# A copy by ScalarE between two products of a Strassen-like down projection

## The chip, the core and the metric

The kernel runs on one core of a Trainium2 chip. The metric is the device time of one execution in microseconds (us); for a kernel that was run several times the median stands. Matmuls run on TensorE (PE in the profile), elementwise work on VectorE (DVE) and ScalarE (ACT), and loads from HBM are issued by SyncE (SP).

## The reference

A decoder trunk for 512 tokens of width 1024, two layers, everything in float32. Each layer is: half an FFN, a mixer (gated linear attention in the first, stick-breaking attention in the second), half an FFN. There are four FFNs, and the change lies in them alone:

```python
D_MODEL, SEQ, DEPTH, D_FF = 1024, 512, 2, 2816

def swiglu(h, w_gate, w_up, w_down):
    return (jax.nn.silu(h @ w_gate) * (h @ w_up)) @ w_down

def reference(x, ...):
    for i in range(DEPTH):
        x = x + 0.5 * swiglu(rmsnorm(x, ffn1_norm[i]), ffn1_w_gate[i], ffn1_w_up[i], ffn1_w_down[i])
        ...  # mixer, added to x
        x = x + 0.5 * swiglu(rmsnorm(x, ffn2_norm[i]), ffn2_w_gate[i], ffn2_w_up[i], ffn2_w_down[i])
    return rmsnorm(x, final_norm)
```

## The kernel before

The residual x lies transposed in SBUF as eight tiles of 128 features by 512 tokens (`xs`). Each float32 operand of a matmul is cut into a high and a low part (`wh`, `wl` for weights): ScalarE casts the high part (L127), VectorE subtracts it to get the low part (L129), and three matmuls (high by high, low by high, high by low) replace one.

An FFN works through its 2816 inner features in six groups. For most of them the gate and up projections (`seven`, matmuls at L689), and for one group the down projection (`seven_down`, matmuls at L368), are done by a scheme with seven half-size products in place of eight (Winograd's form of Strassen's): sums of weight quarters (`sums_12`, `sums_34`; L672 to L679 in `seven`, L352 to L360 in `seven_down`) are multiplied with sums of quarters of the other factor. Other groups go through a plain `down` (tiles `ps_d`).

`seven_down` is called twice in each FFN, as part 0 and part 1 (256 of each 512 output features), so eight times in all. Its two bodies go through seven products, each for m = 0 and m = 1 (128 features each) and each made of 6 matmuls of 128x256. Products are summed in PSUM in six banks: ws[m], zs[m] and qs[m]. After each product but the first (t1, t2 and so on), `add` (L374) has VectorE read the sum from PSUM, scale it by 0.5 and add it into a quarter of the residual. The sum in ws goes on after that: `body_1` puts the product with b11 there, a copy of it goes to zs (L386, ScalarE), then the product with t2 is added; `body_2` adds the product with t3, then works on qs with b22, and then adds the product with t4 to ws. Between t3 and t4 the sum is needed once, for `add(m, 1, 1, ...)`, and a matmul into ws[m] may not start until that has read it.

In `seven` the corresponding sum after t3 is first copied by ScalarE into a tile `u3` in SBUF (L731, tag "c", one buffer), and VectorE adds from there (L732).

The program's order: a queue (`feed`) of entries. At the start of an entry the weights of the next entries are cut as far as four wide buffers allow, and raw weights are loaded up to six entries ahead into two buffers (`raw`, `rawd`). A load into such a buffer starts when the last reader of its former contents is done, which is often the cut of the last quarter (a22, L129 with 128x512). Each engine takes its instructions in order; the order on each is set when the program is built, by a scheduler with its own estimate of times. For the first column block of a `seven` entry that follows other work, ScalarE makes a small cast of 128x128 (L134). Behind `seven_down` part 0 come two pairs of `seven` entries (gate and up); behind part 1 comes a `down`.

Of the kernel before, what the change touches and what calls it, by code (L numbers as in the profile page):

```python
# [10 lines left out]
F32 = mybir.dt.float32  # L11
# [7 lines left out]
P = 128  # L19
# [13 lines left out]
def decoder(ctx: ExitStack, tc: tile.TileContext, a: dict, out: bass.AP):  # L33
    nc = tc.nc
# [12 lines left out]
    def psum(name, tag=None):  # L47
        if tag is None:
            tag = order[turn_[0] % 8]
            turn_[0] += 1  # L50
        return pp.tile([P, T], F32, tag=tag, bufs=banks[tag], name=name)
# [280 lines left out]
    def seven_down(pool, w, r0, hs, part):  # L332

        H = T // 2
        lower, upper = (
            Chunk(w[r0 : r0 + 4 * P, c : c + 256].rearrange("(f p) c -> p f c", p=P), 4, 256)
            for c in (part * 256, 512 + part * 256)
        )  # L340
        lower.few = upper.few = True
        v = {}

        def halves():

            lo, up = (c.load().rearrange("p (c two) d -> p two c d", two=2) for c in (lower, upper))
            return lo[:, 0], lo[:, 1], up[:, 0], up[:, 1]

        def sums_12(_):
            a11, _, a21, a22 = halves()  # L350
            s = v["s12"] = pool().tile([P, 4, 256], F32, tag="s", bufs=4, name="s12")
            nc.vector.tensor_tensor(out=s[:, 0:2], in0=a21, in1=a22, op=ALU.add)  # L352
            nc.vector.tensor_tensor(out=s[:, 2:4], in0=s[:, 0:2], in1=a11, op=ALU.subtract)
            return s

        def sums_34(_):
            a11, a12, a21, _ = halves()
            s = pool().tile([P, 4, 256], F32, tag="s", bufs=4, name="s34")
            nc.vector.tensor_tensor(out=s[:, 0:2], in0=a11, in1=a21, op=ALU.subtract)
            nc.vector.tensor_tensor(out=s[:, 2:4], in0=a12, in1=v["s12"][:, 2:4], op=ALU.subtract)  # L360
            return s

        def prod(ps, w, k0, step, m, b, first):
            for c in range(2):
                bh, bl = hs[c][b]
                wh, wl = (t[:, k0 + step * c, m * P : (m + 1) * P] for t in w)
                for n, (l_, r_) in enumerate(((wh, bh), (wl, bh), (wh, bl))):
                    st["pe"] = nc.tensor.matmul(  # L368
                        ps, l_, r_, start=first and c + n == 0, stop=c == 1 and n == 2, skip_group_check=True
                    ).ins  # L370

        def add(m, up, col, ps):
            x = xs[part * 2 + m + 4 * up][:, col * H : col * H + H]
            nc.vector.scalar_tensor_tensor(out=x, in0=ps, scalar=0.5, in1=x, op0=ALU.mult, op1=ALU.add)  # L374

        def body_1(W):
            ax, s = W
            ws, zs, qs = [], [], []
            for m in range(2):
                ws.append(psum("ps_w")[:, 0:H])  # L380
                prod(ws[m], ax, 0, 2, m, "b11", True)
            for m in range(2):


                zs.append(psum("ps_z")[:, 0:H])
                nc.scalar.copy(zs[m], ws[m])  # L386
            yield
            for m in range(2):
                qs.append(psum("ps_q")[:, 0:H])
                prod(qs[m], s, 0, 1, m, "t1", True)  # L390
                add(m, 1, 1, qs[m])
            yield
            for m in range(2):
                prod(ws[m], s, 2, 1, m, "t2", False)
                add(m, 0, 1, ws[m])
            yield
            for m in range(2):
                prod(zs[m], ax, 1, 2, m, "b21", False)
                add(m, 0, 0, zs[m])
            v["w"], v["q"] = ws, qs  # L400
            yield

        def body_2(W):
            s, a22 = W
            ws, qs = v["w"], v["q"]
            for m in range(2):
                prod(ws[m], s, 0, 1, m, "t3", False)
                add(m, 1, 1, ws[m])
            yield
            for m in range(2):  # L410
                prod(qs[m], s, 2, 1, m, "b22", False)
                add(m, 0, 1, qs[m])
            yield
            for m in range(2):
                prod(ws[m], a22, 0, 1, m, "t4", False)
                add(m, 1, 0, ws[m])
            yield

        feed.q.append(
            Entry([(lower, lambda t: t, 4, 256), (lower, sums_12, 4, 256)], body_1, NEAR, feed.q[-1].place != NEAR)  # L420
        )
        assert not feed.q[-1].lead
        feed.q.append(Entry([(lower, sums_34, 4, 256), (upper, lambda t: halves()[3], 2, 256)], body_2, NEAR))

    def back_tok(w, r0, nf, hs, done):
# [1165 lines left out]
```

## Time and profile before

| | |
|---|---|
| time, median of 3 runs | 1854.52 us (1854.33 to 1854.69) |
| the profiled execution's own time | 1856.01 us |
| its span, first to last instruction | 1854.0 us |
| mean granted TensorE clock | 0.999 |
| TensorE busy | 1828.8 us (99%) |
| VectorE busy | 1476.4 us (80%) |
| ScalarE busy | 1035.9 us (56%) |
| updates of `seven_down` (L374) | 96 on VectorE, 48 of them from ps_w |

Rows of the timeline give the start and the duration of an instruction in us, its engine, its line, the operation, output<-input by tile names with shapes, and in brackets how long the engine sat idle before it and what ended that. A matmul's duration overlaps that of the next: matmuls of 128x256 are issued one after another at much shorter distance than they last. Rows of the groups give the busy time in us, the mean duration in ns, the idle time before and what ended it. The chain of waits is followed back from the last instruction of the span.

### The profile page before, as it was taken

What the parts mean: (1) busy time and instruction counts of PE and PEld (TensorE: products, weight loads), DVE (VectorE), ACT (ScalarE), POOL (GpSimd) and SP (SyncE); (2) the same over time, 40 slices, a digit from 0 to 9 for tenths busy, and PEclk for the clock granted to TensorE, in tenths of its full rate; (3) what the DMA queues carried; (4) which work ended last, traced back from release to release, by engine and by line L of the source; (5) the groups of instructions that cost most, each with busy time, mean ns of one, the idle gap of its engine ahead of it and who ended that gap; (6) DMA issues with size and microseconds to landing.
All of it is one profiled execution on the core that took longest, in us unless ns stands there. A gap on an engine that the chain in (4) does not pass through costs nothing.

```text
span 1854.0 us, 29888 instructions
## 1 busy us (share of the span) xinstructions
PE 1828.8 (99%) x12187; PEld 1649.6 (89%) x12187; DVE 1476.4 (80%) x2336; ACT 1035.9 (56%) x1771; POOL 8.7 (0%) x20
## 2 busy tenths in 40 slices
PE   7999999999999999999999999999999999999998
PEld 6999999889888899999889999998888788999997
DVE  7998776785787989877798997676878779997775
ACT  6555445444555565545565555455878755654454
POOL 0000000100000000000000000000000000000000
PEclk9999999999999999999999999999999999999999
DMA  5333333311223223332233333232221222333321
GB/s 160 114 125 95 118 110 100 98 57 62 69 69 114 91 92 115 115 114 87 82 128 104 98 118 107 95 92 85 69 69 59 67 91 93 112 125 97 121 80 69
DMA packets 177613, 179.16 MB, mean 97 GB/s; under 512 B 4098, under 2 KB 167988, under 8 KB 177476
## 3 DMA queue, kind: packets, MB, share of 16 engines
q1 hardware_dynamic: 176768, 176.18, 30.1%
q8 instruction: 95, 1.56, 0.4%
q0 software_dynamic: 608, 1.05, 0.2%
q14 instruction: 42, 0.34, 0.1%
q10 hardware_dynamic: 100, 0.03, 0.0%
HBM read 175.17 MB, written 2.10 MB: 96 GB/s over the span
## 4 chain that ended last, share of the span: by engine, by line
PE 86%; DVE 9%; DMA 3%; ACT 2%; issue 1%; SPq 0%; DVEq 0%; ACTq 0%
PE ps_d L67 20%; PE ps_f L67 18%; PE ps_w L689 17%; PE ps_q L689 9%; PE ps_t L67 5%; PE ps_z L689 4%; PE ps_b L67 4%; DVE wl L129 3%; DMA raw<-in_ffn_w_gate_dram 2%; PE ps_S L67 1%; PE ps_z L1315 1%; PE ps_bt L67 1%; PE ps_oT L1377 1%; PE ps_w L368 1%; DVE x L374 1%
## 5 line engine op out<-in xcount | busy, mean ns | idle before, releaser
L129 DVE TENSOR_TENSOR wl<-raw,wh 128x1024 fp32r<-128x1024 f32 (+1 forms) x244 | 259.2, 1066 | 89.3 <-ACT wh L127 50.1
L127 ACT CAST wh<-raw 128x1024 fp32r<-128x1024 f32 (+1 forms) x244 | 224.7, 923 | 160.4 <-PE ps_d L67 45.4
L689 PE MATMUL ps_w<-th,wh 128*128 128x256 f32 x864 | 239.6, 277 | 1.4 <-ACT o L719 0.6
L689 PE MATMUL ps_w<-tl,wh 128*128 128x256 f32 x864 | 238.7, 276 | 0.0
L689 PE MATMUL ps_w<-th,wl 128*128 128x256 f32 x864 | 238.6, 276 | 0.0
L129 DVE TENSOR_TENSOR wl<-s,wh 128x1024 fp32r<-128x1024 f32 x160 | 195.4, 1222 | 54.0 <-PE ps_z L689 37.4
L127 ACT CAST wh<-s 128x1024 fp32r<-128x1024 f32 x160 | 168.0, 1050 | 116.8 <-PE ps_d L67 28.9
L67 PE MATMUL ps_d<-hh,wl 128*128 128x512 f32 x544 | 212.1, 390 | 0.0
L67 PE MATMUL ps_d<-hh,wh 128*128 128x512 f32 x544 | 212.1, 390 | 0.0
L67 PE MATMUL ps_d<-hl,wh 128*128 128x512 f32 x544 | 211.6, 389 | 0.0
L67 PE MATMUL ps_f<-xh,wh 128*128 128x512 f32 x448 | 178.9, 400 | 1.6 <-ACT wh L127 1.6
L67 PE MATMUL ps_f<-xl,wh 128*128 128x512 f32 x448 | 175.8, 393 | 0.0
L67 PE MATMUL ps_f<-xh,wl 128*128 128x512 f32 x448 | 175.1, 391 | 0.0
L689 PEld LDWEIGHTS ps_w<-th,wh 128*128 128x128 f32 x864 | 162.3, 188 | 3.0 <-ACT u L731 1.0
L689 PEld LDWEIGHTS ps_w<-th,wl 128*128 128x128 f32 x864 | 162.2, 188 | 0.0
L689 PEld LDWEIGHTS ps_w<-tl,wh 128*128 128x128 f32 x864 | 162.2, 188 | 0.0
L127 ACT CAST wh<-rawd 128x1024 fp32r<-128x1024 f32 (+1 forms) x84 | 84.9, 1012 | 120.3 <-PE ps_d L67 77.4
L323 DVE SCALAR_TENSOR_TENSOR x<-ps_d,x 128x512 f32<-128x512 f32 x152 | 102.9, 688 | 58.6 <-PE ps_d L67 58.0
L129 DVE TENSOR_TENSOR wl<-rawd,wh 128x1024 fp32r<-128x1024 f32 (+1 forms) x84 | 98.3, 1174 | 42.4 <-ACT wh L127 25.1
L67 PEld LDWEIGHTS ps_d<-hl,wh 128*128 128x128 f32 x544 | 102.1, 188 | 21.6
L67 PEld LDWEIGHTS ps_d<-hh,wh 128*128 128x128 f32 x544 | 102.1, 188 | 20.2
L67 PEld LDWEIGHTS ps_d<-hh,wl 128*128 128x128 f32 x544 | 102.1, 188 | 19.7
(323 smaller groups left out, 4847.9 us busy)
## 6 DMA issues: line engine op xcount, KB each, us to landing
raw<-in_ffn_w_gate_dram SPq DMA_DIRECT2D x43, 1024.0 KB, 5.4
raw<-in_ffn_w_up_dram SPq DMA_DIRECT2D x43, 1024.0 KB, 5.4
rawd<-in_ffn_w_down_dram SPq DMA_DIRECT2D x84, 512.0 KB, 3.7
raw<-in_gla_w_in_dram SPq DMA_DIRECT2D x12, 1024.0 KB, 5.3
raw<-in_sb_w_in_dram SPq DMA_DIRECT2D x16, 512.0 KB, 3.8
raw<-in_gla_w_out_dram SPq DMA_DIRECT2D x4, 1024.0 KB, 5.0
raw<-in_sb_w_in_dram SPq DMA_DIRECT2D x4, 1024.0 KB, 5.1
raw<-in_sb_w_out_dram SPq DMA_DIRECT2D x4, 1024.0 KB, 5.0
```

What stands on the lines that cost most here:

```text
L67: st["pe"] = nc.tensor.matmul(ps, l, r, start=first, stop=last).ins
L127: st["cut"] = nc.scalar.copy(h, r).ins
L129: nc.vector.tensor_tensor(out=l, in0=r, in1=h.bitcast(F32), op=ALU.subtract)
L323: nc.vector.scalar_tensor_tensor(out=xs[k], in0=ps, scalar=0.5, in1=xs[k], op0=ALU.mult, op1=ALU.add)
L368: st["pe"] = nc.tensor.matmul(ps, l_, r_, start=first and c + n == 0, stop=c == 1 and n == 2, skip_group_check=True).ins
L374: nc.vector.scalar_tensor_tensor(out=x, in0=ps, scalar=0.5, in1=x, op0=ALU.mult, op1=ALU.add)
L689: st["pe"] = nc.tensor.matmul(o, l_, r_, start=first and j + n == 0, stop=j == 3 and n == 2, skip_group_check=True).ins
L1315: nc.tensor.matmul(o_, l_, r_, start=first, stop=last, skip_group_check=True)
L1377: nc.tensor.matmul(po[e * 64 : e * 64 + 64, j * P : T], self.v[j][:, c : c + 64], self.wt[p, e][bk][:, c0 : c0 + n], start=j == 0, stop=j ...
```

## The change

In `body_2` of `seven_down`, after the product with t3, ScalarE copies the sum from PSUM into a tile `u3` in SBUF, and the update of the residual by VectorE reads `u3`. The tile has two halves, one for each m, and takes the buffer with tag "c" that `seven` uses for its own `u3`; that buffer becomes twice as large. In the built program sixteen copies are added to ScalarE's queue, at each call both together, behind the cast of weight sums that stood there and ahead of the next cast. The t4 matmuls wait for ScalarE where they waited for VectorE. On VectorE the number of instructions is the same; in part 0 of each FFN one sum of weights of the next `seven` (L678), which stood between the two updates that follow t4, is placed later: behind both updates and the next cut (L129, 128x512) in FFNs 1, 3 and 4, behind the two updates and ahead of that cut in FFN 2. TensorE's and SyncE's order is unchanged.

```diff
         def body_2(W):
             s, a22 = W
             ws, qs = v["w"], v["q"]
+
+            u3 = pool().tile([P, 2, H], F32, tag="c", bufs=1, name="u3")
             for m in range(2):
                 prod(ws[m], s, 0, 1, m, "t3", False)
-                add(m, 1, 1, ws[m])
+                nc.scalar.copy(u3[:, m], ws[m])
+                add(m, 1, 1, u3[:, m])
             yield
             for m in range(2):
                 prod(qs[m], s, 2, 1, m, "b22", False)
                 add(m, 0, 1, qs[m])
             yield
             for m in range(2):
                 prod(ws[m], a22, 0, 1, m, "t4", False)
                 add(m, 1, 0, ws[m])
             yield
```

## Prediction

> **What bounds the kernel now.** I read the page first, then TensorE's own waits, then the timelines of the three compute engines around one call of `seven_down`, then the chain of waits behind it. The page's busy times:
>
> ```profile
> PE 1828.8 (99%) x12187; PEld 1649.6 (89%) x12187; DVE 1476.4 (80%) x2336; ACT 1035.9 (56%) x1771; POOL 8.7 (0%) x20
> ```
>
> TensorE sets the time. All that an edit on VectorE or ScalarE can give is a pause of TensorE, so its waits come next (total us, times, longest):
>
> ```profile
> PE ps_w L368 <- DVE x L374: 5.4, 8, 1.1
> ...
> PE ps_w L689 <- ACT u L731: 0.4, 2, 0.2
> ```
>
> L368 is the matmul of `seven_down` and L374 its residual update. There are eight calls (four FFNs, parts 0 and 1), and each pauses once. Where, the first call shows (start, duration of TensorE's matmuls):
>
> ```profile
> 146.41 0.28 PE L368 MATMUL ps_w<-t,wh 128*128 128x256 f32 x1
> ...
> 147.77 0.28 PE L368 MATMUL ps_q<-hl,wh 128*128 128x256 f32 x1
> 149.08 0.38 PE L368 MATMUL ps_w<-nh,wh 128*128 128x256 f32 x1 [1.03 <-DVE x L374]
> 149.30 0.28 PE L368 MATMUL ps_w<-nh,wl 128*128 128x256 f32 x1
> ```
>
> The third product (t3 into ps_w) ends at 146.7, the one with b22 (into ps_q) is issued until 147.77, and the one with t4, which goes on summing in ps_w, starts at 149.08: it may not write before VectorE has read the sum behind t3. VectorE at that time:
>
> ```profile
> 148.00 0.70 DVE L673 TENSOR_TENSOR s<-s,raw 128x512 f32<-128x512 f32 x1
> 148.60 0.76 DVE L374 SCALAR_TENSOR_TENSOR x<-ps_w,x 128x256 f32<-128x256 f32 x2
> 149.26 0.76 DVE L374 SCALAR_TENSOR_TENSOR x<-ps_q,x 128x256 f32<-128x256 f32 x2
> 150.07 0.42 DVE L374 SCALAR_TENSOR_TENSOR x<-ps_w,x 128x256 f32<-128x256 f32 x1
> 150.41 0.68 DVE L678 TENSOR_TENSOR s<-raw 128x512 f32<-128x512 f32 x1
> ...
> 151.40 0.69 DVE L129 TENSOR_TENSOR wl<-raw,wh 128x512 fp32r<-128x512 f32 x1
> ```
>
> The read that TensorE needs comes 1.9 us after its sum was ready, because VectorE is behind with weights (L673 here). ScalarE in the same stretch is not behind:
>
> ```profile
> 145.37 1.05 ACT L127 CAST wh<-s 128x1024 fp32r<-128x1024 f32 x1 [0.26 <-PE ps_z L368]
> 148.13 1.04 ACT L127 CAST wh<-raw 128x1024 fp32r<-128x1024 f32 x1 [1.71 <-PE ps_q L368]
> 150.75 0.62 ACT L127 CAST wh<-raw 128x512 fp32r<-128x512 f32 x1 [1.57 <-PE ps_w L368]
> ```
>
> It idles from 146.42 to 148.13, until b22's product is done.
>
> **The change, part by part.** *The copies.* Sixteen are added (8 calls, m = 0 and 1). The groups of instructions (busy us, mean ns, idle before) hold the nearest rows:
>
> ```profile
> L323 DVE SCALAR_TENSOR_TENSOR x<-ps_d,x 128x512 f32<-128x512 f32 x152 | 102.9, 688 | 58.6 <-PE ps_d L67 58.0
> ...
> L732 DVE TENSOR_TENSOR o<-u,o 128x256 f32<-128x256 f32 x72 | 30.3, 421 | 0.0
> L735 DVE TENSOR_TENSOR o<-ps_q,o 128x256 f32<-128x256 f32 x72 | 30.2, 420 | 0.0
> L473 DVE SCALAR_TENSOR_TENSOR xl<-x,gT,xh 128x512 fp32r<-128x512 f32 x40 | 29.8, 747 | 7.3 <-ACT xh L472 7.3
> ...
> L731 ACT COPY u<-ps_w 128x256 f32<-128x256 f32 x72 | 26.9, 373 | 14.8 <-PE ps_w L689 12.6
> ```
>
> L731 is the same copy in the same shape: 16 x 0.373 = 6.0 us of ScalarE. In the built order both copies of a call stand right behind the cast at 145.37 and ahead of the one at 148.13 (in part 1 likewise between two casts). So in the first call copy m = 0 runs from 146.42 to 146.8 and m = 1, whose product ends at 146.69, to about 147.15. The t4 product could start at 147.77 + 0.11 = 147.88, so copy m = 0 is 1.1 us early, and m = 1, needed 0.7 us later, 1.4 us. What is queued behind them on ScalarE is the cast at 148.13, which waits for TensorE anyway; nothing waits for that. Cost: nothing on the path. Without this idle time the copies would take up to 0.75 us per call.
>
> *The update.* It now reads SBUF. Bounds: no change, by L732 against L735 (421 and 420 ns, SBUF and PSUM source, same shape), and 0.06 us more, which is what the same kind of instruction takes longer with all its operands in SBUF (L473, 747 ns) than with one in PSUM (L323, 688 ns; both 512 columns). I take no change: L732 has the update's shape and operands and differs only in the scale, where L473 reads its scale from a tile and writes another type. Upper end 16 x 0.06 = 1 us of VectorE. The Trainium skill ("Perfetto Trace Analysis", Optimizing Scalar/DVE Operations) gives VectorE some 60 ns of access overhead on SBUF against 125 ns on PSUM, and by it the updates would get cheaper; L732 and L735 do not show that.
>
> *The wait.* TensorE's t4 product now waits for the copy instead of the update, and the copy is early, so the eight pauses go. A pause costs more than its idle time: without it the second t4 matmul would be issued two issue steps of 0.113 us (1.36 us for 12, below) after 147.77, at 148.00, and it is issued at 149.30: 1.30 us for 1.03 of idle, 0.27 more. All eight: 5.4 + 8 x 0.27 = 7.6 us. The four of part 1 are the short ones, 0.60, 0.18, 0.18 and 0.35; the first and the last:
>
> ```profile
> 189.76 0.38 PE L368 MATMUL ps_w<-nh,wh 128*128 128x256 f32 x1 [0.60 <-DVE x L374]
> ...
> 1678.83 0.39 PE L368 MATMUL ps_w<-nh,wh 128*128 128x256 f32 x1 [0.35 <-DVE x L374]
> ```
>
> Part 1 is 1.31 + 4 x 0.27 = 2.4 us, part 0 the other 5.2 us.
>
> *What is late next.* Behind part 0 TensorE meets a second wait, some 19 us on. In the chain that ended last it reads, in the second FFN (start, duration):
>
> ```profile
> 726.18 5.42 DMA raw<-in_ffn_w_gate_dram
> ...
> 736.55 5.45 DMA raw<-in_ffn_w_up_dram
> ...
> 742.23 0.38 ACT u L731
> 742.60 0.04 issue
> 742.65 3.01 PE ps_w L689 x24
> 745.65 1.36 PE ps_q L689 x12
> ```
>
> The cut of the a22 weights (L129, 128x512) frees a raw buffer; that starts a gate load; VectorE's sums of it and the next cut free another buffer for an up load; ScalarE's small cast of that (L134) stands ahead of copy L731 in its queue, and TensorE waits for L731. In the other FFNs the same cast waits for the same load; the first and the last of the four:
>
> ```profile
> 167.71 0.30 ACT L134 CAST w<-raw 128x128 fp32r<-128x128 f32 x1 [0.95 <-DMA raw<-in_ffn_w_up_dram]
> ...
> 1658.52 0.30 ACT L134 CAST w<-raw 128x128 fp32r<-128x128 f32 x1 [1.06 <-DMA raw<-in_ffn_w_up_dram]
> ```
>
> So TensorE is held there already, and what part 0 wins is kept only as far as this chain starts earlier. It starts with the cut at 151.40. Today that waits for ScalarE's cast at 150.75, which waits for the t4 product. With t4 done 1.3 us earlier the cast ends by 150.1, and VectorE decides: its backlog isn't shortened. Behind the ps_q updates (149.26 + 0.76, less the 0.09 by which neighbours overlap) it is free at 149.93; two t4 updates of 0.33 net bring it to 150.6. In the built order L678, which stands between the two t4 updates today, has moved behind the cut in FFNs 1, 3 and 4, so the cut starts at 150.6, 0.80 us earlier than today. In FFN 2 L678 only moves behind the second update and stays ahead of the cut; 0.60 us of the 0.80 is gone and 0.2 is left. Kept of part 0: 3 x 0.80 + 0.2 = 2.6 of 5.2 us.
>
> Behind part 1 come 24 matmuls of a `down`, during which VectorE and ScalarE wait for TensorE; the chain starts anew from TensorE's time there, and I keep all 2.4 us.
>
> *Sum.* 2.6 + 2.4 = 5.0 us. The profiled execution took 1856.0 us with a span of 1854.0; it would come to 1851.0 and 1849.0. It lies 1.5 us above the median of 1854.5, from which the forecast is 1849.5 us, 0.27% less. Some 0.2%, 3.7 us, is what a measurement here can tell from no change.
>
> **The rivals.** *Full gain.* If the loads are not what holds the up cast (a transfer that lands earlier once fewer are in flight), TensorE keeps 7.6 us: 1846.9. Against it is that the chain of waits runs through both loads without slack. 0.10.
>
> *Given back.* VectorE's work does not shrink, and in these stretches it is the engine that is behind. If the weight cuts that follow hold TensorE by what it came early, or the update from SBUF costs its 0.06 us and the cut moves that much less, part 0 keeps nothing and the gain is part 1's at most: 1852.1, down to nothing, 1854.5. For it: the backlog in the VectorE rows. Against it: the list of TensorE's waits names no wait on a weight cut of these stretches, so the cuts have room. 0.24. The Trainium skill ("VectorE: DVE Perf Modes", Rules for kernel authors) points this way: it has a matmul's output copied to SBUF first only if many operations follow, and here one does; by that rule alone the sum would be 0. The rule weighs VectorE's time, while the rows have TensorE waiting for the PSUM bank.
>
> *Slower: copies behind the cast.* If the copies reached ScalarE behind the cast at 148.13, that waits for b22's product and takes 1.04 us, t4 could start only at 148.13 + 1.04 + 0.37 = 149.5, 0.4 us later than today, and in part 1, where a pause costs 2.4 / 4 = 0.6 us and not 1.3, by the same geometry 1.1 us later: 4 x 0.4 + 4 x 1.1 = 6 us, 1860.5. It decides from the point where copy m = 0 ends more than its 1.1 us later than worked out above, and makes the kernel slower from 2.4 us later in part 0 (1.1 + 1.3) and 1.7 in part 1 (1.1 + 0.6). The built order speaks against it. With whatever else keeps ScalarE busy before t3's end, 0.10.
>
> That the change doesn't do what it says is excluded by the built program: t4's first matmuls wait for ScalarE there, and no longer for VectorE.
>
> **How the numbers follow.** The forecast, 1849.5, has 0.56, with 1848.2 to 1850.8 as its own range (the 0.80 us of FFNs 1, 3 and 4 taken as uncertain by 0.3 each, and part of the 1 us of VectorE). The range for 8 in 10 takes in the full gain, 1846.9, and the part-1-only case up to 1852.8; left out are the slower case and the half of "given back" that ends close to today's time. Faster by over 0.2% (under 1850.8): 0.56 + 0.10 = 0.66; within: 0.24; slower: 0.10.
>
> **What would show it.** Right: TensorE's list of waits has no entry L368 on the update; t4 follows b22 at one issue step; sixteen copies of about 0.37 us in ScalarE's idle time; the wait on L731 19 us behind part 0 has grown from 0.4 us to about 3 us in all (by the 2.6 us that part 0 doesn't keep); the a22 cut stands 0.8 us closer behind the t3 product in three FFNs and 0.2 in one. Wrong: an L368 wait on the copy; no longer L731 wait and 7 us gained; or new waits of TensorE on L129 in place of the old ones.

## Result and the profile after

| | before | after |
|---|---|---|
| median, beside each other on one chip (7 runs each) | 1854.52 us (1853.08 to 1855.45) | 1848.36 us (1846.99 to 1850.55) |
| ratio after / before, 95% interval | | 0.9968 [0.9957, 0.998] |
| the profiled execution's own time, its span | 1856.01, 1854.0 us | 1849.38, 1847.5 us |

The change makes the kernel faster by 3.7 to 8.0 us (by the interval), 6.2 us by the medians; repeated on another chip (below) it gave 0.9972 [0.9962, 0.9982], 4.5 us by the medians. The forecast was 1849.5 us. Lines behind 404 have moved by 3: L731 of before is L734 of after, L689 is L692, L678 is L681. The copy is L410.

The busy times of after, from the page, and TensorE's waits (total us, times, longest us):

```profile
PE 1827.2 (99%) x12187; PEld 1649.9 (89%) x12187; DVE 1475.1 (80%) x2336; ACT 1040.5 (56%) x1787; POOL 8.7 (0%) x20
...
PE ps_w L692 <- ACT u L734: 2.3, 4, 0.7
...
PE ps_w L692 <- ACT ps_z L716: 0.6, 3, 0.2
...
PE ps_w L368 <- ACT ps_z L386: 0.3, 1, 0.3
```

VectorE's busy time is nearly that of before (1475.1 against 1476.4 us), ScalarE has 16 instructions more, and TensorE executes as many matmuls as before. The entry `L368 <- DVE x L374` (5.4 us in 8) is gone, and none on L410 has come. In its place the wait at the copy in `seven` has grown from 0.4 us in 2 to 2.3 us in 4, one in each FFN. TensorE in the first call, part 0 of the first FFN (start, duration):

```profile
146.98 0.28 PE L368 MATMUL ps_q<-hh,wl 128*128 128x256 f32 x1
147.09 0.28 PE L368 MATMUL ps_q<-hl,wh 128*128 128x256 f32 x1
147.21 0.28 PE L368 MATMUL ps_w<-nh,wh 128*128 128x256 f32 x1
147.32 0.28 PE L368 MATMUL ps_w<-nh,wl 128*128 128x256 f32 x1
```

The product with t4 (ps_w) follows the one with b22 (ps_q) at one issue step. ScalarE and VectorE in the same stretch:

```profile
145.64 0.78 ACT L410 COPY u<-ps_w 128x256 f32<-128x256 f32 x2
147.41 1.05 ACT L127 CAST wh<-raw 128x1024 fp32r<-128x1024 f32 x1 [0.99 <-PE ps_q L368]
148.76 0.62 ACT L127 CAST wh<-raw 128x512 fp32r<-128x512 f32 x1 [0.31 <-PE ps_w L368]
```

```profile
147.95 0.75 DVE L374 SCALAR_TENSOR_TENSOR x<-u,x 128x256 f32<-128x256 f32 x2
...
149.29 0.75 DVE L374 SCALAR_TENSOR_TENSOR x<-ps_w,x 128x256 f32<-128x256 f32 x2
149.95 0.68 DVE L129 TENSOR_TENSOR wl<-raw,wh 128x512 fp32r<-128x512 f32 x1
150.55 0.69 DVE L681 TENSOR_TENSOR s<-raw 128x512 f32<-128x512 f32 x1
```

Both copies lie in ScalarE's idle time and are over at 146.42, 0.79 us before t4's first matmul. VectorE reads `u` only at 147.95, so its read, had TensorE still to wait for it, would hold t4 as before. The cut (L129, 128x512) starts at 149.95, with L681 behind it. In the second FFN L681 stands ahead of the cut:

```profile
721.49 0.68 DVE L681 TENSOR_TENSOR s<-raw 128x512 f32<-128x512 f32 x1
722.09 0.68 DVE L129 TENSOR_TENSOR wl<-raw,wh 128x512 fp32r<-128x512 f32 x1
```

The groups of instructions of after (busy us, mean ns):

```profile
L410 ACT COPY u<-ps_w 128x256 f32<-128x256 f32 x16 | 5.9, 368 | 0.6 <-PE ps_w L368 0.3
```

```profile
L374 DVE SCALAR_TENSOR_TENSOR x<-ps_w,x 128x256 f32<-128x256 f32 x32 | 12.3, 411 | 0.0
...
L374 DVE SCALAR_TENSOR_TENSOR x<-u,x 128x256 f32<-128x256 f32 x16 | 6.0, 415 | 0.0
```

And 19 us behind that call, ScalarE and then TensorE:

```profile
166.47 0.30 ACT L134 CAST w<-raw 128x128 fp32r<-128x128 f32 x1 [1.69 <-DMA raw<-in_ffn_w_up_dram]
166.68 0.36 ACT L734 COPY u<-ps_w 128x256 f32<-128x256 f32 x1
```

```profile
167.09 0.39 PE L692 MATMUL ps_w<-th,wh 128*128 128x256 f32 x1 [0.69 <-ACT u L734]
```

The small cast L134 waits for the up load (1.69 us, before: 0.95), the copy L734 stands behind it, and TensorE, earlier than before, now idles 0.69 us there.

How long each of the eight calls of `seven_down` takes on TensorE, from the start of its first L368 matmul to that of its last, is read off the timelines (us):

| trace | part 0: FFN 1, 2, 3, 4 | part 1: FFN 1, 2, 3, 4 |
|---|---|---|
| before | 10.70, 10.82, 10.70, 10.82 | 11.83, 9.87, 9.87, 10.04 |
| after | 9.41, 9.41, 9.41, 9.41 | 10.37, 9.41, 9.41, 9.85 |

84 matmuls, issued 0.1133 us apart, take 9.4 us from first to last. In part 0 the four calls became shorter by 1.29, 1.41, 1.29 and 1.41 us, 5.40 in all. Part 1 of the first FFN holds another wait, for a late load, in both traces (last section).

### The profile page after: what moved, and what is told of

The parts are those of the page before. It is cut to its first block, busy times and chain, and to the rows that moved or that the text cites. A ratio compares the mean times of both kernels' runs of the same rounds, so it can differ in the third digit from the quotient of the medians.

```text
span 1847.5 us, 29912 instructions
## 1 busy us (share of the span) xinstructions
PE 1827.2 (99%) x12187; PEld 1649.9 (89%) x12187; DVE 1475.1 (80%) x2336; ACT 1040.5 (56%) x1787; POOL 8.7 (0%) x20
## 4 chain that ended last, share of the span: by engine, by line
PE 89%; DVE 5%; DMA 3%; ACT 1%; issue 1%; SPq 0%; ACTq 0%; DVEq 0%
PE ps_d L67 20%; PE ps_w L692 18%; PE ps_f L67 18%; PE ps_q L692 9%; PE ps_t L67 5%; PE ps_z L692 5%; PE ps_b L67 4%; DVE wl L129 2%; PE ps_w L368 2%; DMA raw<-in_ffn_w_gate_dram 2%; PE ps_S L67 1%; PE ps_z L1318 1%; PE ps_bt L67 1%; DMA raw<-in_ffn_w_up_dram 1%; PE ps_oT L1380 1%; PE ps_T L1365 1%
## 5 line engine op out<-in xcount | busy, mean ns | idle before, releaser
L129 DVE TENSOR_TENSOR wl<-raw,wh 128x1024 fp32r<-128x1024 f32 (+1 forms) x244 | 258.2, 1062 | 89.8 <-ACT wh L127 56.4
L692 PE MATMUL ps_w<-th,wh 128*128 128x256 f32 x864 | 239.6, 277 | 2.9 <-ACT u L734 2.3
L692 PE MATMUL ps_w<-tl,wh 128*128 128x256 f32 x864 | 238.8, 276 | 0.0
L692 PE MATMUL ps_w<-th,wl 128*128 128x256 f32 x864 | 238.7, 276 | 0.0
L129 DVE TENSOR_TENSOR wl<-s,wh 128x1024 fp32r<-128x1024 f32 x160 | 195.0, 1220 | 50.4 <-PE ps_z L692 34.7
L692 PEld LDWEIGHTS ps_w<-th,wh 128*128 128x128 f32 x864 | 162.3, 188 | 4.4 <-ACT u L734 3.1
L692 PEld LDWEIGHTS ps_w<-tl,wh 128*128 128x128 f32 x864 | 162.3, 188 | 0.0
L692 PEld LDWEIGHTS ps_w<-th,wl 128*128 128x128 f32 x864 | 162.2, 188 | 0.0
L129 DVE TENSOR_TENSOR wl<-rawd,wh 128x1024 fp32r<-128x1024 f32 (+1 forms) x84 | 98.0, 1170 | 41.7 <-ACT wh L127 24.1
```

What stands on the lines that cost most here:

```text
L129: nc.vector.tensor_tensor(out=l, in0=r, in1=h.bitcast(F32), op=ALU.subtract)
L692: st["pe"] = nc.tensor.matmul(o, l_, r_, start=first and j + n == 0, stop=j == 3 and n == 2, skip_group_check=True).ins
```

## Experiments

The theory: TensorE gains because its t4 product no longer waits until VectorE has read the PSUM bank; it keeps all of that in part 1, and in part 0 only as much as the chain of cut, gate load, up load and small cast L134 starts earlier. Rivals: VectorE gains because it reads SBUF; the copies cost ScalarE time on the path; the second wait doesn't bind; what part 0 keeps comes from the other place of one weight sum in VectorE's order (L678 of before), and not from the bank.

**The copies are made and not read.**

```diff
-                add(m, 1, 1, u3[:, m])
+                add(m, 1, 1, ws[m])
```

> The changed kernel, but the update behind t3 reads the sum in PSUM again; ScalarE's sixteen copies are still made and nobody reads them. VectorE's order is that of the kernel before. Bank release (my theory: the gain is TensorE no longer waiting for VectorE's read of ps_w ahead of t4): the eight pauses L368 <- DVE x L374 are back (about 5.4 us of idle), the sixteen copies take 6 us of ScalarE's idle time and cost nothing, and the time is that of the kernel before, within 1 us; the list of TensorE's waits again has about 0.4 us on the copy in seven. Cheaper update (the gain comes from VectorE reading SBUF): also the time of before. So this run by itself tells what the copies cost: if they cost anything, it is above before by up to 6 us. Copies behind the cast (the slower rival of the prediction) would show as a wait L368 <- ACT u L410.

Measured: 1853.31 us against 1854.66 for before on that chip, ratio 0.9995 [0.9987, 1.0004]. TensorE's waits, and the group of the copies:

```profile
PE ps_w L368 <- DVE x L374: 4.2, 6, 1.0
...
PE ps_w L692 <- ACT u L734: 0.3, 1, 0.3
```

```profile
L410 ACT COPY u<-ps_w 128x256 f32<-128x256 f32 x16 | 5.9, 369 | 0.5
```

The pauses are back: six of the eight stand in the list, and all eight calls are about as long as before (10.65 to 10.77 us in part 0, 9.85 to 10.06 in part 1). The gain is gone, and sixteen copies by themselves cost nothing that shows. As the updates behind t3 read PSUM here, this run alone doesn't rule out the cheaper update; the 415 ns of `x<-u` beside 411 of `x<-ps_w` above do. It doesn't test the last rival either: VectorE's order is that of before again, with the weight sum back between the two updates behind t4.

**The copy in one part only.** `e_part0` makes and reads it for `part == 0`, `e_part1` for `part == 1`; the other part updates from `ws[m]`. The lines of `e_part0` against the changed kernel (the tile `u3`, too, is then made in that part only):

```diff
-                nc.scalar.copy(u3[:, m], ws[m])
-                add(m, 1, 1, u3[:, m])
+                if part == 0: nc.scalar.copy(u3[:, m], ws[m])
+                add(m, 1, 1, u3[:, m] if part == 0 else ws[m])
```

> The copy and the update from it only in part 0 of each FFN (four calls); part 1 as before. Bank release with a second wait behind it: 5.3 us of pauses go, TensorE gives about 3 us of it back at the copy in seven that follows (its waits grow from 0.4 us to over 2), and 2.2 to 2.6 us are kept: about 1852. Without a second wait (the prediction's rival of the full gain): 5.2 us, about 1849.3. If the gain came from cheaper updates of VectorE, half of the change's gain, 3 us.

> The copy and the update from it only in part 1 of each FFN (four calls); part 0 as before. Bank release: the four short pauses of part 1 go (1.3 us of idle, 2.4 to 2.8 us with their restarts) and all of it is kept, because VectorE and ScalarE wait for TensorE in the down that follows: about 1852, and the waits on the copy in seven stay at about 0.4 us. If pauses cost only their idle time: 1.3 us, about 1853.2. If the gain of the change is all of part 0: 0.

Measured: part 0 alone 1852.36 us, ratio 0.9986 [0.9977, 0.9995]; part 1 alone 1852.49 us, 0.9995 [0.9986, 1.0004]; before on that chip 1854.66. TensorE's waits with part 0 alone, then with part 1 alone:

```profile
PE ps_w L692 <- ACT u L734: 1.8, 4, 0.6
...
PE ps_w L368 <- DVE x L374: 0.7, 3, 0.4
```

```profile
PE ps_w L368 <- DVE x L374: 4.1, 4, 1.2
...
PE ps_w L692 <- ACT u L734: 0.5, 2, 0.2
```

The wait at L734 comes with part 0's pauses going (1.8 us in 4) and stays away with part 1's (0.5 us in 2). Part 0 alone is faster by 2.3 us (by the interval 0.9 to 4.3), as the theory has it, and not by 5.2. For part 1 alone the interval reaches from a gain of 2.6 us to a loss of 0.7: by time it is open, by the trace its four pauses are gone (the four that are left, 4.1 us, are those of part 0).

**The small cast out of the copy's way.** L134 is put behind the large cast of the same load, so that it is no longer ahead of L734 (L731); the edit is made on the changed kernel twice and on the kernel before once.

```diff
-                        nc.scalar.copy(first, r[:, 0, 0:P])
+                        with tc.issue_after(st["cut"]): nc.scalar.copy(first, r[:, 0, 0:P])
```

> The changed kernel, with ScalarE's small cast L134 put behind the large cast of the same load, so that it no longer stands ahead of the copy L734 in ScalarE's queue; nothing else moves. If L734 is late because L134 waits there for the up load (the prediction's chain), TensorE's waits L692 <- ACT u L734 (2.3 us in 4) go, and with restarts of 0.27 us each up to 3.4 us could be won; as the first matmuls that need the up weights come later and the loads themselves are not earlier, I expect FFN 1 to give back what it wins and the other three to keep up to 0.8 each: about 2 us less than the changed kernel, near 1846. If L734 is late for its own reason (the t3 product of seven or ScalarE's other work), the waits stay and the time is that of the changed kernel. If the loads are the bound throughout, the wait reappears on L134's or L127's output, and the time is unchanged or worse.

> The changed kernel once more, on the chip on which the next two run, so that they can be compared with it directly, and for a second trace. Expected: 1848.4 within 1 us, L368 waits gone again, about 2 us of waits on the copy L734. Waits at single loads (the start, the gate load ahead of part 1 in the first FFN, the load around 660 us) may differ from the first trace: those that do are not the change's.

> The changed kernel with the small cast L134 behind the large cast of the same load, a second time, beside the changed kernel on the same chip. If the time that part 0 gave back sits in the queue position of L134, it is about 2 us (1 to 3) below the changed kernel; if the loads bound this stretch whatever the order, the two are equal within 0.5 us.

> The kernel before (no copy in down by seven products) with the small cast L134 put behind the large cast of the same load. There TensorE waited on the copy in seven for only 0.4 us in 2, with some 0.64 us on L716/L719 near 660 us: with its pauses at t4, it reached that copy late enough. If L734 is a wait that the change brought to the surface, this edit is worth at most 0.4 + 2 x 0.27 = 0.9 us here against about 2 us or more on the changed kernel, and the eight pauses L368 <- DVE x L374 stay (5.4 us). If it gains as much here as there, the two edits are independent, and part 0's gain was not given back at L134.

> The kernel before, once more, for a second trace of it. In its first trace a gate load ahead of part 1 of the first FFN landed 1.8 us later than in the traces of other versions, and there was a wait of 0.64 us at 659 us. If those are chance, they are missing here or stand elsewhere, while the eight pauses L368 <- DVE x L374 are there again with 5 to 5.5 us; if they belong to the kernel before, they come again.

Measured: the edit on the changed kernel 1846.76 us, 0.9962 [0.995, 0.9975], and on the next chip 1847.73 us, 0.9963 [0.995, 0.9975], where the changed kernel took 1849.26 us, 0.9972 [0.9962, 0.9982]; on the kernel before 1853.46, 0.9992 [0.9983, 1.0001], with the pauses at t4 still there (4.5 us in 5). Before took 1854.66 us on the first chip and 1853.80 on the second. ScalarE in the second trace of the edit on the changed kernel:

```profile
163.02 2.14 ACT L127 CAST wh<-s 128x1024 fp32r<-128x1024 f32 x2
165.53 0.37 ACT L734 COPY u<-ps_w 128x256 f32<-128x256 f32 x1 [0.36 <-PE ps_w L692]
```

L734 now waits for TensorE, and no entry `L692 <- ACT u L734` is left; the changed kernel's second trace has 1.3 us in 4. So the position of L134 in ScalarE's queue, and not the loads' end as such, is where most of what part 0 gave back was lost. How much it was, the traces tell better than the times: from the first matmul of each call of part 0, the start of the first L719 behind t4 and that of the third L734 behind it (copies of ScalarE that follow TensorE's products; L716 and L731 in before) are compared with the first trace of before, summed over the four FFNs (us):

| trace | won at t4 of part 0 | given back behind it | kept |
|---|---|---|---|
| after | 5.41 | 2.77 | 2.64 |
| after, second trace | 5.41 | 2.05 | 3.36 |
| part 0 alone | 4.91 | 3.13 | 1.78 |
| after with L134 behind (two traces) | 5.41, 5.41 | 0.81, 0.83 | 4.60, 4.58 |
| copies unread; part 1 alone; before, second trace | 0.24, -0.07, -0.57 | 0.34, 0.79, 1.04 | -0.10, -0.87, -1.61 |

The last row shows the scatter where part 0 has nothing to win: against the second trace of before every figure of "kept" would be 1.6 us larger, 1.3 of it in the first FFN. By the table the edit adds 1.2 to 2.0 us in part 0; the clock shows 1.5 (1847.73 against 1849.26) with overlapping intervals. On the kernel before, where I had expected 0.9 us at most, it shows 0.3 us by the medians and 1.5 by the ratio, whose interval holds no change. That it is worth more after the change than before it isn't shown. In both traces with it the calls of part 1 took 9.58 to 9.99 us instead of 9.41 to 9.85 (the call with the late load left out), which eats part of it. By the medians it is the fastest version that was run.

The second trace of before has the pauses again (4.9 us in 7), but not the idle time of 0.64 us that the first has at 670 us (not at 659, where the expectation puts it), and, at 1853.2, the smaller span.

**Copies that end later.** Each copy is made three, and six times.

```diff
-                nc.scalar.copy(u3[:, m], ws[m])
+                for _ in range(3): nc.scalar.copy(u3[:, m], ws[m])
```

> The changed kernel with each of the sixteen copies made three times (96 copies less 48 of 0.372 us more on ScalarE; neighbours start 0.28 us apart). By the prediction's slack (copy m = 0 ends 1.1 us, m = 1 1.4 us before t4 needs it) two more of m = 0 end 0.56 us later and m = 1 1.1 us later, both still in time: no wait L368 <- ACT u L410, and the time of the changed kernel, 1848.4 to 1849.3, within 1 us. If the copies had cost what they take (ScalarE on the path), 32 x 0.28 = 9 us more.

> The changed kernel with each copy made six times; in the built order the last one of m = 1 then stands behind the large cast that waits for b22's product. This is the slower rival of the prediction made real for m = 1: the cast takes 1.05 us after the copies before it, so that the last copy ends some 2.2 us after t4's matmuls of m = 1 could have started. Expected: no wait at t4's m = 0 or one under 0.3 us, one of about 2.2 us at m = 1 in each of the eight calls (16 to 20 us in TensorE's list, L368 <- ACT u L410), with 0.27 us more each; part of it comes off because TensorE no longer waits at the copy L734 behind part 0. About 1866 us (1862 to 1870), slower than before. If the wait on ScalarE could be hidden the way the rest of ScalarE's work is, the time stays under 1854.

Measured: three times 1848.93 us, 0.9974 [0.9963, 0.9984]; six times 1868.8 us (one run), with before at 1854.45. The 48 copies take 15.5 us of ScalarE and none of the path; a call takes 9.40 to 9.55 us. With six, TensorE's wait, ScalarE and TensorE in the first call:

```profile
PE ps_w L368 <- ACT u L410: 14.1, 16, 1.3
```

```profile
145.86 3.26 ACT L410 COPY u<-ps_w 128x256 f32<-128x256 f32 x11
148.90 1.15 ACT L127 CAST wh<-raw 128x1024 fp32r<-128x1024 f32 x1
149.85 0.48 ACT L410 COPY u<-ps_w 128x256 f32<-128x256 f32 x1
```

```profile
148.89 0.38 PE L368 MATMUL ps_w<-nh,wh 128*128 128x256 f32 x1 [1.30 <-ACT u L410]
150.38 0.39 PE L368 MATMUL ps_w<-nh,wh 128*128 128x256 f32 x1 [0.52 <-ACT u L410]
```

The last copy starts only when the cast is through, and t4's second half waits for it; its first half waits too, which I had not expected, since by that row (148.89, the eleven copies end at 149.12) its last copy is one of the last of the eleven. A call takes 11.81 to 12.21 us, 20.3 more over the eight than at 9.41, and the time is 19.9 us above that with three. The slower rival's mechanism is real: the gain hangs on the copies' place ahead of that cast. Its price of 6 us isn't tested by this run, in which both halves of t4 wait.

## Why the prediction was right

- **The sum.** 5.0 us, 1849.5 us: measured 6.2 and 4.5 us, 1848.4 and 1849.3. From the first trace of after, the terms come to 2.64 us kept of part 0 and 1.8 of part 1, 4.4 us; from the second, 3.36 and as much, 5.2. The spans of the first two traces differ by 6.5 us, more than the sum, but 0.68 of that is there at 74 us, ahead of any edited work, and 0.9 more comes with the idle time at 670 us of before, which no other trace has in that size, the second of before included: chance of that execution.
- **The pauses.** Part 0 5.2 us: the calls became 5.40 shorter, idle time and 0.27 us each included. Part 1 2.4 us was somewhat too much. FFN 2 and 3 gave the 0.46 each that the step gives (9.87 to 9.41). FFN 4 should have given 0.62 and gave 0.19 (10.04 to 9.85), since its matmuls were issued more slowly; in the trace with three copies it takes 9.41 and gives 0.63. FFN 1 should have given 0.87; against the traces without the copy there and without the late load (10.02 to 10.11) the 9.41 of the second trace are 0.6 to 0.7. Together some 1.8 us. What part 1 won was kept where the traces let it be followed: in the second FFN TensorE's lead over the first trace of before grows from 3.60 us (751 us) to 4.06 (761 us) and is 4.08 at 1040 us.
- **Kept of part 0.** 2.6 of 5.2 us: 2.64 of 5.41, and 3.36, 2.71 (three copies) and 1.78 (part 0 alone) in other traces. From the first matmul of the call to the cut it is 10.91, 11.39, 10.80 and 11.04 us in after, 11.67, 11.79, 11.67 and 11.78 before: 0.76, 0.40, 0.87 and 0.74 closer for a forecast of 0.80, 0.2, 0.80 and 0.80. The mechanism is the one named, but the sum agrees better than its parts: kept were 0.25, 0.62, 0.96 and 0.81 us in the four FFNs, and 0.97, 0.44, 1.21 and 0.74 in the second trace, so that in the first trace the errors of FFN 1 and FFN 2 offset each other. And by the working itself 0.60 of each 0.80 is not the bank's: it is the weight sum L678 (L681 of after), which the scheduler put behind the cut. No run kept it in its old place. The nearest is FFN 2, where it stays ahead of the cut: there 0.62 and 0.44 us were kept. How much of part 0's gain would be left in the other three FFNs without that move stays open; the pauses themselves do not hang on it, since t4 begins ahead of the updates (147.21 against 147.95).
- **The second wait.** I wrote that the wait on the copy grows to about 3 us. It is 2.3 and 1.3 us: I had booked as idle time all that is given back, while the restarts of 0.27 us are part of it, and there are two more of them than in the first trace of before (four waits for two).
- **Copies and update.** The slack of 1.1 and 1.4 us was there: by the row of the two copies (145.64, 0.78 us for both, 0.37 for one) m = 0 ended at 146.01 and t4 began at 147.21, 1.2 us later; m = 1 ended at 146.42 and was needed six issue steps after 147.21, at 147.89, 1.5 us later. Three copies each still fitted. The update got no cheaper: 415 ns from `u` beside 411 from ps_w in after, 424 beside 421 with part 0 alone. The 421 ns of the first trace of before against 415 is no gain, for VectorE's updates differ by as much between executions of one program: they take 415 ns from ps_w in the second trace of before. The Trainium skill ("Perfetto Trace Analysis", Optimizing Scalar/DVE Operations) has VectorE's access to SBUF cheaper by 65 ns than to PSUM; `x<-u` and `x<-ps_w` in one trace don't show that (415 and 411 ns).
- **The rivals.** Given back: in part, as forecast. By the Trainium skill ("VectorE: DVE Perf Modes", Rules for kernel authors), which copies a matmul's output to SBUF first only where many operations follow, the sum would have been 0. Here one operation follows, and the copy pays (ratio 0.9968): not through VectorE, but because TensorE gets its bank back. Slower: the copies stood where the built order has them; the price had a small slip (149.54 against 149.08 is 0.46 us a call, not 0.4), which changes nothing in the sum.

## What to carry to other kernels

Where TensorE goes on summing in a PSUM bank that a busy engine must read in between, let an idle engine copy the sum out: the gain is the pause and its restart (0.27 us beyond the idle time here), and it is there only as long as the copy stands in the idle engine's queue ahead of work that waits for TensorE. Before booking the gain, follow TensorE to its next wait; what arrives early at a queue that a load holds is given back there, and moving one small instruction out of the way can release it, as the traces with L134 behind show. Compare two traces of the same program before explaining a microsecond between two programs.

## What the hardware showed that I had not expected

Two differences between executions, each as large as the terms of this sum.

A gate load of the first FFN that lands late. SyncE's issue of it, and VectorE's first sum of it, in the first trace of before:

```profile
172.54 0.63 SPq L92 DMA_DIRECT2D raw<-in_ffn_w_gate_dram  x1
```

```profile
180.55 0.69 DVE L672 TENSOR_TENSOR s<-raw 128x512 f32<-128x512 f32 x1 [2.18 <-DMA raw<-in_ffn_w_gate_dram]
```

and in the second trace of after:

```profile
171.12 0.37 SPq L92 DMA_DIRECT2D raw<-in_ffn_w_gate_dram  x1
```

```profile
177.33 0.69 DVE L675 TENSOR_TENSOR s<-raw 128x512 f32<-128x512 f32 x1 [0.60 <-DMA raw<-in_ffn_w_gate_dram]
```

From issue to the first sum it is 8.0 us here and 6.2 there. Late (7.5 to 8.0 us, with an issue of 0.63 to 0.79 us) are both traces of before, the first of after and that with six copies; the second of after and the seven other traces have 6.0 to 6.5 us and an issue of 0.37 to 0.43. The changed kernel stands in both groups, so it goes with the execution. With it the call of part 1 is longer by 1.0 us in after (10.37 against 9.41 in the second trace) and by 1.8 in before (11.83 against 10.02 in the trace of before with L134 behind).

Matmuls of one shape at two issue distances. In part 1 of the fourth FFN, after, and the changed kernel with three copies:

```profile
1670.12 0.28 PE L368 MATMUL ps_w<-nl,wh 128*128 128x256 f32 x1
1670.23 0.28 PE L368 MATMUL ps_w<-t,wh 128*128 128x256 f32 x1
1670.35 0.28 PE L368 MATMUL ps_w<-t,wl 128*128 128x256 f32 x1
1670.47 0.28 PE L368 MATMUL ps_w<-t,wh 128*128 128x256 f32 x1
```

```profile
1668.08 0.28 PE L368 MATMUL ps_w<-t,wl 128*128 128x256 f32 x1
1668.19 0.28 PE L368 MATMUL ps_w<-t,wh 128*128 128x256 f32 x1
1668.31 0.28 PE L368 MATMUL ps_w<-nh,wh 128*128 128x256 f32 x1
1668.42 0.28 PE L368 MATMUL ps_w<-nh,wl 128*128 128x256 f32 x1
```

0.118 against 0.113 us in the mean, without a wait, and with a granted clock of 1.00 for both stretches. Slow stretches last from some us up to 41 and stand at other places in other executions. Of the 7647 matmuls of this shape, 340 to 986 in a trace follow at 0.1155 to 0.121 us; by an estimate from these counts (4.4 ns each) that is 1.5 to 4.3 us an execution. The first trace of before has the fewest, its second the most. What sets them off stays open.
